# Gated linear attention in a two-layer backbone: running, rescaled q and k instead of operands rebuilt from the gate at each block size

## Chip, cores and metric

The kernel runs on one core of a Trainium2 chip, as one launch in float32 (the large projections split each float32 operand into a high and a low part and multiply three times). The metric is the device time of that launch in microseconds: median 3550.06 us over three runs, 3549.6 to 3558.3 us.

## The reference, cut to what matters

Two layers, each with one combined input projection, four mixers on 256 columns each (mLSTM, Hyena convolution, gated linear attention "GLA", windowed attention) and one output projection, over 256 context and 2048 latent tokens. The change concerns GLA. For each of 4 heads of 64 channels, in both directions in time:

```
b = jnp.cumsum(ab, axis=2)
decay = jnp.exp(jnp.where(tri, b[:, :, :, None, :] - b[:, :, None, :, :], -jnp.inf))
att = jnp.einsum('bhtd,bhsd,bhtsd->bhts', qb, kb, decay)
o = o_inter + jnp.einsum('bhts,bhse->bhte', att, vb)
```

The decay differs per channel, so `att` is not one product of q and k. A kernel can split a chunk into blocks: between two neighbouring blocks of cc tokens the decay factors at their border into one factor for the later tokens and one for the earlier, and a product of q and k, each multiplied by its factor, gives that off-diagonal square. With cc = 64, 32, ... 1 all pairs of a 128-token chunk are covered; the diagonal is q times k itself (counted twice, once per direction).

## The kernel before, in words

Tokens go in 18 tiles of 128. Each layer runs its mixers one after the other; beside the mixing of one, the PE works on the projection of the next. A helper `paced` ties the projection's matmuls to the mixer's: the projection's k-step i waits for a "mark" (a matmul of the mixer) whose number grows in proportion, so the projection is spread over the mixing. A scheduler then writes out one fixed order of instructions per engine, and every engine works its list strictly in order. GLA mixing (`gla_mix`, L934, `gla_chunk`, L954) runs beside the first part of the mLSTM projection (`mlstm_proj`, 27648 of its 46080 cost units; three matmuls of 256 columns, called one group below, are 64 units). The rest of that projection runs beside `mlstm_pre` (gates and states), which follows GLA.

`gla_chunk` handles one 128-token chunk: 18 of them in layer 0, 16 in layer 1. `streams` lets two chunks be written at a time, the second starting when the first has made 8 steps. In a chunk, `bt` holds the cumulative gate for both directions (4 blocks of 128: direction by head pair) and `qk` q and k. For each block size cc = 64 to 2, one level:

- L995 subtracts the gate at the block border from `bt` into `D` (512 elements per partition; DVE for three levels, POOL for three);
- L999 to L1001 exponentiate it into `ex` with the sign that each quarter needs (ACT, 256 + 128 + 128 elements);
- L1002 multiplies `ex` by `qk` (DVE, 512 elements);
- L1008, L1011 or L1015 multiply k by q on the PE. For cc below 32 that is 16 matmuls of 64x32 by 64x32, four column groups by two row groups of the array.

No level reads what another level wrote. Levels cc = 1 and 0 (the diagonal) use L980 to L989. Then the six small results are merged by masks into `D32` (L1022, L1024) and copied into the 128x128 `S` (L1027); L1029 and L1031 make `qi`, q times the decay from the chunk's ends; L1038 to L1042 are the output matmuls; `hh` is copied out of PSUM (L216) and normalised (`head_norm`: POOL square L661, DVE L662, then `rsqrt_mean` L225 to L230 with two ACT steps, L664), multiplied by the SiLU gate and transposed out (L696).

Of the kernel before, what the change touches and what calls it, by code (L numbers as in the profile page):

```python
# [41 lines left out]
def consts():  # L42
# [114 lines left out]
class Net:  # L157
# [796 lines left out]
    def gla_chunk(self, p, c, sb, ngb, sel):  # L954
        nc = self.nc
        qk = p.tile([P, 4, P], F32, tag="qk", name="qk")
        nc.sync.dma_start(out=qk, in_=self.qk_src(self.g_qk, c))
        bt = p.tile([P, 4, P], F32, tag="bt", name="bt")
        nc.sync.dma_start(out=bt, in_=self.g_bt[c])
# [11 lines left out]
        vC = [pS[:, :, x:x + 64].rearrange("p e (m t) -> p e m t", m=2) for x in (256, 320, 384, 448)]  # L971
        vD = [pS[:, 0, x:x + 4].rearrange("p (m e) -> p e m", m=2) for x in (0, 4)]
        for lv, cc in enumerate((64, 32, 16, 8, 4, 2, 1, 0)):
            ex = p.tile([P, 4, P], F32, tag="ex", name="ex", bufs=4)
            if cc < 2:
                if cc:
                    t2 = lambda x, i: x.rearrange("p j (n x) -> p j n x", x=2)[:, :, :, i]
                    D = p.tile([P, 512], F32, tag="D", name="D")
                    Dv = D[:, :256].rearrange("p (j n) -> p j n", j=4)
                    nc.gpsimd.tensor_sub(out=Dv, in0=t2(bt, 1), in1=t2(bt, 0))  # L980
                    for i in range(2):
# [35 lines left out]
            if cc == 32:  # L1017
                nc.scalar.copy(out=S, in_=vS)
# [719 lines left out]
```

## Time and profile before

| | |
|---|---|
| median of 3 runs | 3550.06 us (3549.6 to 3558.3) |
| profiled execution: span, first to last instruction | 3548.5 us |
| what lies around the span | the median run is 1.6 us longer than this span, the fastest 1.1 us |
| busy share PE / DVE / ACT / POOL | 91% / 61% / 40% / 37% |
| mean granted clock of the PE | 0.941 of 2.4 GHz |
| GLA mixing in layer 0 | from 1047 to 1400 us |
| GLA mixing in layer 1 | from 2827 to 3118 us |

The 91% of the PE is an average over stages and counts matmuls whose ends are modelled; a granted clock of 0.5 means that the PE ran at 1.2 GHz. A stage is judged by its own windows: how much of it the PE was busy, at which clock, and which wait ended last there.

### The profile page before, as it was taken

How to read it: one execution, taken by the hardware profiler on the slowest of the kernel's cores; microseconds unless marked ns; L12 is line 12 of the kernel's file. 1: busy time of each engine (PE TensorE's matmuls, PEld its weight loads, DVE VectorE, ACT ScalarE, POOL GpSimd, SP SyncE). 2: the span in 40 equal slices, each digit the busy share in tenths (PEclk: the TensorE clock that was granted, in tenths of full speed). 3: DMA queues.
4: the chain of work that ended last, by engine and by line, in shares of the span. 5: the costliest groups of instructions: out<-in, count | busy, mean ns of one | idle time of the engine just before them, and what ended most of it. 6: DMA issues, size and time to landing. Idle time of an engine off the chain costs nothing. (4 is left out here: it accounts for less than half of the span.)

```text
span 3548.5 us, 68631 instructions
## 1 busy us (share of the span) xinstructions
PE 3243.7 (91%) x24673; PEld 2694.4 (76%) x24673; DVE 2178.6 (61%) x5322; ACT 1424.0 (40%) x4044; POOL 1311.0 (37%) x1561
## 2 busy tenths in 40 slices
PE   6989999899998989988898999998999998887998
PEld 4778878698886778876678677776988876776776
DVE  6733565553458686579888425664533478946887
ACT  5513444332544443233435324443325445522333
POOL 3611111232126565245555421112331266723555
PEclk8999999999998988989899999999999999997999
DMA  6374443684354432475434474435753432237443
GB/s 247 105 209 121 113 116 105 181 248 128 120 174 139 129 116 69 145 221 161 147 124 136 114 209 129 117 98 161 234 153 108 134 89 88 82 100 199 156 146 106
DMA packets 532007, 503.65 MB, mean 142 GB/s; under 512 B 113808, under 2 KB 457677, under 8 KB 531667
## 3 DMA queue, kind: packets, MB, share of 16 engines
q1 hardware_dynamic: 531667, 499.26, 47.2%
q8 instruction: 195, 3.19, 0.4%
q14 instruction: 145, 1.19, 0.1%
HBM read 333.18 MB, written 165.92 MB: 141 GB/s over the span
## 5 line engine op out<-in xcount | busy, mean ns | idle before, releaser
L480 PE MATMUL pp<-w,hi 128*128 128x256 f32 (+2 forms) x1984 | 593.5, 301 | 25.1 <-ACT w L425 11.4
L482 PE MATMUL pp<-w,hi 128*128 128x256 f32 (+2 forms) x1984 | 595.1, 301 | 6.2 <-POOL w L426 6.0
L483 PE MATMUL pp<-w,ho 128*128 128x256 f32 (+2 forms) x1984 | 590.9, 298 | 3.4 <-POOL ho L380 3.2
L463 PE MATMUL pp<-hi,w 128*128 128x512 f32 (+1 forms) x1328 | 526.6, 397 | 5.0 <-ACT w L425 3.2
L466 PE MATMUL pp<-hi,w 128*128 128x512 f32 (+1 forms) x1328 | 515.8, 390 | 1.9 <-POOL w L426 1.7
L465 PE MATMUL pp<-ho,w 128*128 128x512 f32 (+1 forms) x1328 | 515.9, 389 | 0.0
L480 PEld LDWEIGHTS pp<-w,hi 128*128 128x128 f32 x1984 | 388.0, 196 | 45.2 <-ACT w L425 16.9
L482 PEld LDWEIGHTS pp<-w,hi 128*128 128x128 f32 x1984 | 388.8, 196 | 22.3 <-issue 10.3
L483 PEld LDWEIGHTS pp<-w,ho 128*128 128x128 f32 x1984 | 389.4, 196 | 16.7 <-issue 9.0
L426 POOL TENSOR_TENSOR w<-raw,w 128x256 fp32r<-128x256 f32 (+2 forms) x256 | 197.3, 788 | 525.1 <-ACT w L425 487.8
L463 PEld LDWEIGHTS pp<-hi,w 128*128 128x128 f32 x1328 | 257.5, 194 | 62.1 <-issue 9.2
L466 PEld LDWEIGHTS pp<-hi,w 128*128 128x128 f32 x1328 | 253.4, 192 | 53.1 <-POOL w L426 3.3
L465 PEld LDWEIGHTS pp<-ho,w 128*128 128x128 f32 x1328 | 255.5, 192 | 45.3 <-issue 3.2
L1639 PE MATMUL pp<-woh,w 128*128 128x512 f32 x544 | 235.7, 434 | 30.7 <-ACT pp L1643 17.5
L1640 PE MATMUL pp<-wol,w 128*128 128x512 f32 x544 | 224.0, 413 | 0.0
L1641 PE MATMUL pp<-woh,w 128*128 128x512 f32 x544 | 221.2, 416 | 2.1 <-POOL w L1628 2.1
L216 DVE COPY st<-pp 128x256 f32<-128x256 f32 (+2 forms) x152 | 79.5, 523 | 199.2 <-PE pp L483 98.6
L1002 DVE TENSOR_TENSOR ex<-ex,qk 128x512 f32<-128x512 f32 x204 | 180.1, 885 | 30.1 <-ACT ex L1001 27.1
L218 ACT COPY st<-pp 128x256 f32<-128x256 f32 (+2 forms) x152 | 68.6, 451 | 260.8 <-PE pp L483 139.0
L1208 POOL TENSOR_TENSOR sg<-sg,gt 128x256 f32<-128x256 f32 x34 | 25.0, 737 | 396.1 <-ACT sg L654 357.7
L652 ACT ACTIVATE sg<-sg 128x256 f32<-128x256 f32 (+1 forms) x120 | 60.6, 505 | 241.3 <-DVE sg L651 225.5
L425 ACT CAST w<-raw 128x256 fp32r<-128x256 f32 (+2 forms) x256 | 96.3, 407 | 150.4 <-DMA raw<-in_w_in_dram 90.8
(591 smaller groups left out, 7327.0 us busy)
## 6 DMA issues: line engine op xcount, KB each, us to landing
raw<-in_w_in_dram SPq DMA_DIRECT2D x96, 256.0 KB
q<-d_tq SPq DMA_DIRECT2D x68, 256.0 KB
E<-d_mM SPq DMA_DIRECT2D x68, 256.0 KB
d_yraw<-st SPq DMA_DIRECT2D x64, 256.0 KB
raw<-in_w_ada_dram SPq DMA_DIRECT2D x64, 256.0 KB
wsho<-d_aT SPq DMA_DIRECT2D x34, 384.0 KB
kl<-d_tk SPq DMA_DIRECT2D x28, 384.0 KB
d_gbt<-bt SPq DMA_DIRECT2D x36, 256.0 KB
```

The lines of the kernel that those rows point to most:

```text
L425: nc.scalar.copy(out=t[:, 0, :n], in_=raw[:, i, :n])
L426: nc.gpsimd.tensor_sub(out=t[:, 1, :n], in0=raw[:, i, :n], in1=t[:, 0, :n])
L463: mm = nc.tensor.matmul(out=ps[:, :n], lhsT=a, rhs=hi[:, k], start=(k == 0), stop=False)
L465: nc.tensor.matmul(out=ps[:, :n], lhsT=a, rhs=lo[:, k], start=False, stop=False)
L466: nc.tensor.matmul(out=ps[:, :n], lhsT=b, rhs=hi[:, k], start=False, stop=(k == KD - 1))
L480: mm = nc.tensor.matmul(out=ps[:, :n], lhsT=a, rhs=wk[k][:, 0, :n], start=(k == 0), stop=False)
L482: nc.tensor.matmul(out=ps[:, :n], lhsT=a, rhs=wk[k][:, 1, :n], start=False, stop=False)
L483: nc.tensor.matmul(out=ps[:, :n], lhsT=b, rhs=wk[k][:, 0, :n], start=False, stop=(k == KD - 1))
L1002: nc.vector.tensor_mul(out=ex, in0=ex, in1=qk)
L1639: nc.tensor.matmul(out=ps, lhsT=ak[k][:, 0], rhs=hi[:, k], start=(k == order[0]), stop=False)
L1640: nc.tensor.matmul(out=ps, lhsT=ak[k][:, 0], rhs=lo[:, k], start=False, stop=False)
L1641: nc.tensor.matmul(out=ps, lhsT=ak[k][:, 1], rhs=hi[:, k], start=False, stop=(k == order[-1]))
```

## The change

One tile `X` of four quarters (256 elements each: two head pairs by 128 tokens) replaces the levels' separate operands: at first q, k, k, and q times the whole-block factor of the backward direction; quarter 0 is multiplied by the factor of the forward direction. All factors of all levels come from one small tile `A` (1016 elements), filled by seven POOL subtractions of gate values one block apart and two ACT exponentials per chunk. Then the levels run smallest block first: the PE multiplies what `X` holds, and afterwards two DVE multiplications in place scale `X` by the factors of this block size, so that it is ready for the next larger one. For cc = 2 to 32 an ACT copy first gathers the two kinds of k into one tile `KM` (one buffer). After the last level, quarters 0 and 3 of `X` are q times the decay from both chunk ends, so `qi` with its exponential and product goes. The copies of `D32` into `S` move from DVE to ACT. X loads q once and k twice (three DMAs for one), and the gate tile has a gap of one column per block.

```
+        for cc in (1, 2, 4, 8, 16, 32, 64):
+            nc.gpsimd.tensor_sub(out=grid(A, off, (508, 2), (254, 2), (1, n)), in0=grid(T, cc, (257, 2), (129, 2), (cc, n)),
+                                 in1=grid(T, 0, (257, 2), (129, 2), (cc, n)))
+        for d in range(2):
+            nc.scalar.activation(out=A[:, 508 * d:508 * d + 508], in_=A[:, 508 * d:508 * d + 508], func=ACTF.Exp, scale=0.125 * d - 0.0625)
...
+        nc.gpsimd.tensor_mul(out=qk, in0=quad(0), in1=quad(1))
...
+        for d in (1, 0):
+            nc.vector.tensor_mul(out=grid(X, 768 * d, (128, 2), (1, P)), in0=grid(X, 0, (128, 2), (1, P)), in1=grid(A, 508 * d, (254, 2), (1, P)))
-        for lv, cc in enumerate((64, 32, 16, 8, 4, 2, 1, 0)):
+        for cc in (1, 2, 4, 8, 16, 32, 64):
...
-                (nc.vector if lv in (1, 3, 5) else nc.gpsimd).tensor_sub(out=Dv, in0=bv, in1=bv[:, :, cc - 1].unsqueeze(2).to_broadcast([P, 512 // x, x]))
-                nc.scalar.activation(out=self.pair(ev[:, :h, lo], cc), in_=self.pair(Dv[:, :h, lo], 256 + cc), func=ACTF.Exp, scale=0.0625)
-                nc.scalar.activation(out=ev[:, h:, lo], in_=Dv[:, h:, lo], func=ACTF.Exp, scale=-0.0625)
-                nc.scalar.activation(out=ev[:, h:, hi], in_=Dv[:, :h, hi], func=ACTF.Exp, scale=-0.0625)
-                nc.vector.tensor_mul(out=ex, in0=ex, in1=qk)
+            if cc in (1, 64):
+                KM = quad(1)
+            else:
+                KM = p.tile([P, 256], F32, tag="KM", name="KM", bufs=1)
+                nc.scalar.copy(out=grid(KM, 0, (x, 256 // x), (cc, 2), (1, cc)), in_=grid(X, 256, (x, 256 // x), (256 + cc, 2), (1, cc)))
...
+                w = max(32, x)
+                for j in range(0, P, w):
+                    kk = Kr[:, o:o + w]
+                    qq = grid(Xr, o, (x, w // x), (768 + cc, 2), (1, cc))
+                    if cc == 32:
+                        mk = nc.tensor.matmul(out=vS[j:j + 64, e, m, j:j + 64], lhsT=kk, rhs=qq, start=True, stop=True)
+                    else:
+                        mk = nc.tensor.matmul(out=vC[cc][j:j + 32, e, m], lhsT=kk, rhs=qq, start=True, stop=True, tile_position=(64 * e, j))
...
+            if cc < 64:
+                for i, u in ((0, 0), (2, 1)):
+                    t = grid(X, 256 * i + cc * u, (128, 4), (x, b), (1, cc))
+                    nc.vector.tensor_mul(out=t, in0=t, in1=grid(A, f + 1 - u, (254, 4), (2, b), (0, cc)))
+            if cc == 1:
+                nc.vector.tensor_copy(out=D32, in_=vC[1])
+                nc.vector.copy_predicated(out=D32, mask=self.msk[:, 4].unsqueeze(1).unsqueeze(1).to_broadcast([P, 2, 2, 32]),
...
+        nc.scalar.copy(out=S, in_=vS)
...
-            nc.vector.tensor_copy(out=S[x, :, :, x], in_=D32[x])
-        nc.scalar.activation(out=qi, in_=bt, func=ACTF.Exp, scale=0.0625)
-        nc.gpsimd.tensor_mul(out=qv, in0=qv, in1=qk[:, 0:2].unsqueeze(1).to_broadcast([P, 2, 2, P]))
+            nc.scalar.copy(out=S[x, :, :, x], in_=D32[x])
```

The scheduler's lists change with it. On DVE, between the copy of one chunk's `hh` out of PSUM (L216) and the work on the next, layer 0 before:

```order
L995 TENSOR_TENSOR D<-bt 128x512
L216 COPY hh<-pse 128x256
L984 TENSOR_TENSOR ex<-ex 128x256
L1002 TENSOR_TENSOR ex<-ex,qk 128x512 x2
L995 TENSOR_TENSOR D<-bt 128x512
L662 TENSOR_REDUCE ss<-sq 128x4
L1022 COPY D_12752<-psA 128x128
```

The same place in the changed kernel (L998 sets up `X`, L1031 scales it after a level, L1037 and L1038 begin `D32`):

```order
L1044 COPY_PREDICATED D_12597<-msk,psC 128x128 x4
L216 COPY hh<-pse 128x256
L998 TENSOR_TENSOR X<-X,A 128x256
L662 TENSOR_REDUCE ss<-sq 128x4
L998 TENSOR_TENSOR X<-X,A 128x256
L225 TENSOR_SCALAR v<-ss 128x4
L228 SCALAR_TENSOR_TENSOR t<-ss 128x4
L229 TENSOR_TENSOR t<-t,v 128x4
L230 SCALAR_TENSOR_TENSOR ss<-t,ss 128x4
L664 TENSOR_TENSOR hh<-hh,ss 128x256
L1031 TENSOR_TENSOR X<-X,A 128x256 x2
L1037 COPY D_12796<-psA 128x128
```

Before, work of the next chunk's levels stands ahead of the copy of `hh`; now the next chunk's first multiplication stands behind it, and the first scaling of `X` behind the norm of the chunk before.

On PE, the levels of one chunk in layer 0 of the changed kernel (L1024 are the matmuls of a level, L463 to L466 one group of the projection):

```order
L1024 MATMUL psC<-X,KM 32x32 x16
L463 MATMUL pp<-hi_678,w 128x512
L465 MATMUL pp<-ho_679,w 128x512
L466 MATMUL pp<-hi_678,w 128x512
L1024 MATMUL psC<-X,KM 32x32 x16
L463 MATMUL pp<-hi_678,w 128x512
L465 MATMUL pp<-ho_679,w 128x512
L466 MATMUL pp<-hi_678,w 128x512
L1022 MATMUL psC<-X,KM 64x64 x8
```

Before, the matmuls of several levels of a chunk could stand together, as the 48 of three levels here in layer 0, behind the last output matmul of the chunk before:

```order
L1042 MATMUL pse<-sb_10802,qi 128x128
L1015 MATMUL psA<-ex 32x32 x48
L463 MATMUL pp<-hi_678,w 128x512
L465 MATMUL pp<-ho_679,w 128x512
L466 MATMUL pp<-hi_678,w 128x512
L463 MATMUL pp<-hi_678,w 128x512
```

Now two levels are never adjacent: three matmuls of 512 columns, or six of 256, stand between them.

On ACT, the end of one chunk and the start of the next in the changed kernel (L1005 copies into `KM`, L1047 the four copies into `S`, L984 the exponentials of the next chunk, L652 to L654 the sigmoid):

```order
L1005 COPY KM<-X 128x256 x4
L218 COPY st<-pp 128x4x64
L1042 COPY S<-psC 128x512
L1047 COPY S<-D_12995 32x4x32 x4
L984 ACTIVATE A<-A 128x508 x2
L226 ACTIVATE t<-v 128x4
L227 ACTIVATE ss<-t 128x4
L1005 COPY KM<-X 128x256
L652 ACTIVATE sg<-sg 128x256
```

What moved: the four `S` copies now stand on ACT between the last level and the output matmuls.

## Rows read from the trace of the kernel before

**Rows 1.** Busy time by stretch: PE, PEld, DVE, ACT, POOL, granted clock, DMA, GB/s.
```profile
1072.00:1400.00 328.00, 288.96 (x3997) 236.22 (x3988) 251.01 (x501) 148.64 (x511) 211.21 (x243) 0.85 0.39 116
2849.00:3118.00 269.00, 232.11 (x3408) 200.48 (x3382) 224.77 (x425) 130.57 (x445) 187.90 (x217) 0.92 0.29 87
1400.00:1518.00 118.00, 112.70 (x928) 97.91 (x927) 60.01 (x206) 21.21 (x56) 24.49 (x30) 1.00 0.45 133
3118.00:3250.00 132.00, 113.23 (x907) 97.48 (x905) 65.22 (x205) 26.52 (x66) 34.39 (x38) 0.93 0.54 154
```

**Rows 2.** Timeline, DVE: first and last hh copy of each layer (start, duration).
```profile
1071.64 0.43 DVE L216 COPY hh<-pse 128x256 f32<-128x256 f32 x1 [1.71 <-PE pse L1042]
...
1400.34 0.42 DVE L216 COPY hh<-pse 128x256 f32<-128x256 f32 x1 [5.61 <-PE pse L1042]
...
2848.88 0.42 DVE L216 COPY hh<-psm 128x256 f32<-128x256 f32 x1 [1.38 <-PE psm L1042]
...
3118.12 0.42 DVE L216 COPY hh<-psm 128x256 f32<-128x256 f32 x1
```

**Rows 3.** Waits of PE, 1040 to 1400 us, longest first: total, times, longest.
```profile
PE psC L1015 <- DVE ex L1002: 9.2, 5, 3.7
```

**Rows 4.** Timeline, PE, 2.4 GHz: one level; output matmuls; first and last of seven projection matmuls.
```profile
1313.33 0.36 PE L1015 MATMUL psC<-ex 64*32 64x32 f32 x32
...
1310.13 0.56 PE L1041 MATMUL pse<-v,S 128*128 128x64 f32 x4
...
1311.42 0.44 PE L1042 MATMUL pse<-sb,qi 128*128 128x128 f32 x2
...
1317.12 0.28 PE L482 MATMUL pp<-w,hi 128*128 128x256 f32 x1
...
1317.83 0.28 PE L482 MATMUL pp<-w,hi 128*128 128x256 f32 x1
```

**Rows 5.** Line L661 (POOL), line L999 and L1000 (ACT): ns min/median/max.
```profile
L661 POOL TENSOR_TENSOR sq<-hh x68: 606/614/1595, 1073.0 to 3522.9; 128x256 f32<-128x256 f32 x68
L999 ACT ACTIVATE ex<-D x204: 398/417/455, 1044.9 to 3101.4; 128x256 f32<-128x256 f32 x102
L1000 ACT ACTIVATE ex<-D x204: 290/294/325, 1045.2 to 3101.7; 128x128 f32<-128x128 f32 x102
```

**Rows 6.** Timeline, DVE: the norm of one chunk with no other work between.
```profile
1401.49 0.42 DVE L662 TENSOR_REDUCE ss<-sq 128x4 f32<-128x256 f32 x1 [0.40 <-POOL sq L661]
...
1403.21 0.42 DVE L664 TENSOR_TENSOR hh<-hh,ss 128x256 f32<-128x256 f32 x1
```

**Rows 7.** Timeline, DVE: two independent 256-element operations, and five masked copies in a row.
```profile
2984.33 0.41 DVE L664 TENSOR_TENSOR hh<-hh,ss 128x256 f32<-128x256 f32 x1
2984.66 0.41 DVE L216 COPY hh<-psm 128x256 f32<-128x256 f32 x1
...
3107.73 1.65 DVE L1024 COPY_PREDICATED D<-msk,psC 128x128 f32<-128x128 uint8 x5
```

**Rows 8.** Timeline, PE, 1.2 GHz: one level; first and last output matmuls.
```profile
1120.51 0.47 PE L1015 MATMUL psA<-ex 64*32 64x32 f32 x32 [1.72 <-DVE ex L1002]
...
1249.85 0.95 PE L1041 MATMUL pse<-v,S 128*128 128x64 f32 x4
...
1252.30 0.74 PE L1042 MATMUL pse<-sb,qi 128*128 128x128 f32 x2
```

**Rows 9.** Tile ex, whole run: ns min/median/max, first and last start.
```profile
L1002 DVE TENSOR_TENSOR ex<-ex,qk x204: 673/693/1779, 1045.8 to 3103.0; 128x512 f32<-128x512 f32 x102
L1008 PE MATMUL psA<-ex x136: 272/272/579, 1047.1 to 3073.8; 64*128 64x128 f32 x136
```

**Rows 10.** Groups by shape, 2827 to 3118 us, DVE: busy us, mean ns.
```profile
L1002 DVE TENSOR_TENSOR ex<-ex,qk 128x512 f32<-128x512 f32 x95 | 87.5, 924 | 6.7 <-ACT ex L1001 6.2
```

**Rows 11.** Line L984 (DVE, 256 elements, right behind POOL's L983): ns min/median/max.
```profile
L984 DVE TENSOR_TENSOR ex<-ex x34: 410/956/1511, 1056.7 to 3105.0; 128x256 f32<-128x256 f32 x34
```

**Rows 12.** Tile ex, 2815 to 2860 us: first GLA matmul of layer 1.
```profile
L1008 PE MATMUL psA<-ex x16: 272/272/373, 2827.0 to 2858.1; 64*128 64x128 f32 x16
```

More of the change, by code (lines that the diff above doesn't have):

```diff
@@ L952, in pair, with grid, gla_chunk @@
         return bass.AP(ap.tensor, ap.offset, [ap.ap[0], [step, 2], *ap.ap[1:]])
[L954 to L959, printed above, removed]
+    @staticmethod
+    def grid(ap, off, *dims):
+        return bass.AP(ap.tensor, ap.offset + off, [ap.ap[0], *[list(d) for d in dims]])
+    def gla_chunk(self, p, c, sb, T, ngb, sel):
+        nc, grid = self.nc, self.grid
+        X = p.tile([P, 4 * 256], F32, tag="X", name="X")
+        src = self.qk_src(self.g_qk, c)
+        quad = lambda i: X[:, 256 * i:256 * i + 256]
+        nc.sync.dma_start(out=grid(T, 0, (129, 4), (1, P)), in_=self.g_bt[c])
+        for i in range(3):
+            nc.sync.dma_start(out=quad(i).rearrange("p (m t) -> p m t", m=2), in_=src[:, 2:] if i else src[:, :2])
         v = p.tile([P, 256], F32, tag="v", name="v")
@@ new lines, in gla_chunk @@
+        vC = {cc: pS[:, :, x:x + 64].rearrange("p e (m t) -> p e m t", m=2) for cc, x in ((16, 256), (8, 320), (4, 384), (2, 448), (1, 64))}
+        vD = pS[:, 0, 0:4].rearrange("p (m e) -> p e m", m=2)
+        qk = p.tile([P, 256], F32, tag="hh", name="qk")
+        nc.gpsimd.tensor_mul(out=qk, in0=quad(0), in1=quad(1))
+        for m in range(2):
+            mk = nc.tensor.matmul(out=pS[:, 0, 2 * m:2 * m + 2], lhsT=qk[:, P * m:P * m + P], rhs=sel, start=True, stop=True)
+        self.marks.append(mk)
@@ L1020, in gla_chunk @@
             yield
         nc.sync.dma_start(out=gt, in_=self.g_g[c][:, :256])
[L1022 to L1024 removed]
+        nc.scalar.copy(out=S, in_=vS)
+        for i, cc in enumerate((16, 8, 4, 2)):
+            nc.vector.copy_predicated(out=D32, mask=self.msk[:, i].unsqueeze(1).unsqueeze(1).to_broadcast([P, 2, 2, 32]), data=vC[cc])
@@ L1037, in gla_chunk @@
             po = pf.rearrange("p (h d) -> p h d", h=2)
-            nc.tensor.matmul(out=pf, lhsT=qi[:, 2 + m], rhs=sb[:, 0, m].rearrange("p h d -> p (h d)"), start=True, stop=False)
+            nc.tensor.matmul(out=pf, lhsT=X[:, 768 + P * m:768 + P * m + P], rhs=sb[:, 0, m].rearrange("p h d -> p (h d)"), start=True, stop=False)
             for h in range(2):
@@ L1041, in gla_chunk @@
                 nc.tensor.matmul(out=po[:, h], lhsT=S[:, h, m], rhs=v[:, 64 * g:64 * g + 64], start=False, stop=False, skip_group_check=True)
-            nc.tensor.matmul(out=pf, lhsT=qi[:, m], rhs=sb[:, 1, m].rearrange("p h d -> p (h d)"), start=False, stop=True)
+            nc.tensor.matmul(out=pf, lhsT=X[:, P * m:P * m + P], rhs=sb[:, 1, m].rearrange("p h d -> p (h d)"), start=False, stop=True)
         self.copy(hh.rearrange("p h d -> p (h d)"), pq.rearrange("p m n -> p (m n)"))
```

82 lines of the change are left out of this document (31 added, 51 removed).

## Prediction, made before the changed kernel was run

> **What bounds the kernel now.** I read the busy time by stretch first, because the change touches only the two GLA stages. In the one of layer 0 the PE is busy 289 of 328 us at a mean clock of 0.85, in layer 1 232 of 269 us at 0.92; behind each stage it is busy 96% and 86% at 1.00 and 0.93 [rows 1]. So the GLA stages are where PE time is lost, to waits and to the slower clock. DVE and POOL together are busy 462 of 328 us and 413 of 269 us there [rows 1], so they often run at once. Then the copies of `hh` give the pace: 17 chunks in 1400.34 - 1071.64 us, 19.34 us each, in layer 0; 15 in 3118.12 - 2848.88, 17.95 us each, in layer 1 [rows 2]. The PE's waits inside a stage are short, the longest kind 9.2 us in total [rows 3]: no single chain holds the old stage; the levels are independent and fill each other's gaps.
>
> **The change, part by part.** Per chunk it removes, on ACT, three exponentials for each of six levels and `qi`; on DVE, three subtractions of 512 elements, six products of 512 and four copies; on POOL, three subtractions, `qi` and the two levels below 2. It adds twelve DVE products of 256 elements, two of 128 and two of 256 to start, five ACT gathers, two ACT exponentials, four ACT copies, seven POOL subtractions of 1016 elements in all. All engines but the PE have less to do. The PE gets one more level of 16 matmuls and 8 smaller ones for the 4 of cc = 64, and 2 diagonal matmuls in place of 4: about 0 in sum (a level is 0.36 us, [rows 4]). What costs is that the levels are now a chain: PE reads `X`, DVE scales it, ACT gathers `KM`, PE reads again. And by the lists in the section on the change, the next chunk starts on DVE only behind the copy of `hh`. So the pace of a chunk is the length of its chain, P, from one copy of `hh` to the next. The projection cannot fill more than its pace: counted in the list, a steady chunk has 17 to 19 groups, 51 to 57 matmuls of 0.118 us, about 6.5 us, and GLA itself has some 5.5 us on the PE.
>
> P at the fast clock with nothing in the way, handovers between engines 0.05 us each:
> - copy of `hh` 0.42; POOL square 0.61 [rows 5]; the norm from L662 to the end of L664, 1403.21 + 0.42 - 1401.49 = 2.14 [rows 6]; one start product between, 0.3; handovers: 3.6 us.
> - two products of 256 elements: 0.41 each, the second 0.33 later [rows 7], 0.75 us. Level 1 on the PE is hidden beside the norm.
> - levels 2 to 32: gather 0.41, the time of L999 for 256 elements [rows 5]; PE 0.36 [rows 4]; products 0.75; handovers 0.15: 1.67 us, times 5 = 8.35. The sigmoid's three steps on ACT delay the second gather by about 0.35 (an estimate: three of about 0.41 and a copy, less one level). 8.7 us.
> - level 64: PE 0.46 (estimate: two column widths of a level), two products of 128 elements 0.5 (estimate from [rows 7]), four masked copies at 1.65 / 5 = 0.33 each [rows 7], four ACT copies 0.29 with 0.2 between their starts, 0.9 [rows 5], handovers: 3.4 us.
> - output matmuls 1310.13 to 1311.86, 1.73 us [rows 4], and the handover: 1.8 us.
>
> Sum: 18.2 us. The projection's groups between two levels take 6 x 0.118 = 0.7 us and fit beside the 1.3 us in which DVE and ACT work.
>
> Two costs come on top. **The clock:** at P = 18.2 the PE would be busy some 12 of 18 us, less than in the old stage where 88% still meant a mean clock of 0.85 [rows 1]. At 1.2 GHz a level takes 0.47 and the output 1252.30 + 0.74 - 1249.85 = 3.2 us [rows 8], so 7 x 0.11 + 1.46 = 2.2 us more. The ends are 0 and 2.2; I take half, 1.1. **DVE beside POOL:** L1002 takes 673 ns alone and 924 on average in layer 1, where POOL is busy 70% [rows 9, 10, 1], 37% longer. POOL will have about 7 us per chunk (norm and gate as now, seven subtractions, one product), 35%, so half of that on about 6.2 us of products: 1.1 us. The lower end is 0. The upper is six products that each meet a POOL operation at the price of L984, 956 instead of 410 ns [rows 11]: 3.3 us. I take 1.1, as the average holds many meetings. P = 20.4 us.
>
> On these meetings the Trainium skill ("SBUF — State Buffer", "SBUF: two separate sides") says that DVE with two SBUF inputs and GpSimd exclude each other from the port for a whole instruction, which speaks for the upper end: by it the sum would be that of the third rival below. The 956 ns of L984 agree with it [rows 11].
>
> The strided reads of level 1 and 2 are bounded by L999, which reads pairs of pieces, and by twice that; 0.4 us in one level, which I leave at 0 since the level 1 read lies beside the norm. The two extra DMAs of a chunk on SP are issued a chunk ahead (two `X` buffers) and cost nothing while a transfer needs less than 18 us.
>
> **Sum.** Start: between the first GLA matmul and the second chunk the list now holds 75 groups of 272 columns (0.377 us, [rows 4] by the columns) in layer 0, 76 in layer 1, with GLA's own 5.5 us 33.8 and 34.2 us to the first copy of `hh`; it was 1071.64 - 1047.1 = 24.5 and 2848.88 - 2827.0 = 21.9 [rows 2, 9, 12]. GLA begins 8 and 4 groups earlier, 3.0 and 1.5 us. Net 6.3 + 10.8 = 17 us. Pace: 17 (P - 19.34) + 15 (P - 17.95). Given back: at the last level's matmul 488 groups of the projection are done instead of 422, and 490 instead of 448 in layer 1; 108 x 0.355 = 38 us less remain for the stage behind [rows 4, 1]. There DVE has only 60 and 65 us of work in 118 and 132 us, but its gate steps are a chain of their own, so I count three quarters, 28 us (ends 15 and 38). Together 32 P - 609; break-even at P = 19.0. With P = 20.4: +44 us. Against the profiled execution, 3548.5 + 44 = 3592.5 us of span; the median lies 1.6 us above that execution, so **3594 us**.
>
> **Rivals.**
> - *Faster.* The old stage is held by DVE and POOL getting in each other's way; with half the POOL work this ends, the clock stays up, P = 18.2: 582 - 609 = -27, 3523 us. For it: 924 against 673 ns, and all of DVE, ACT and POOL get less. Against: 12 of 18 us of PE work. It decides below P = 18.7. Chance 0.22.
> - *No change.* Only one of the two costs arises: P = 19.3 or less, 617 - 609 = +8, about 3555 us. Chance 0.13.
> - *Much slower.* POOL meets the products at the upper price and the clock is half the time low: P = 18.2 + 3.3 + 1.1 = 22.6, +114, 3664 us. For it: POOL's subtractions for the next chunk stand in the middle of this chunk's levels. Chance 0.12.
>
> **How the numbers follow.** A measurement of this kernel can tell 0.3%, 10.7 us, from no change. The forecast, P from 19.4 to 21.9, has 0.53, and 3562 to 3642 us. Faster by over 0.3% is the first rival, 0.22; within it the second, 0.13; slower 0.53 + 0.12 = 0.65. The range goes to 3524 below, which leaves out half of the first rival, and to 3642 above, which leaves out most of the third: some 2 in 10. The signs hold 0.65 to 0.22, and the forecast's own range is 3562 to 3642.
>
> **What would show it.** Right: copies of `hh` 20 to 21 us apart in both layers; DVE waiting for PE (L1024) and ACT (gathers) before L1031, PE waiting for ACT `KM` at every level; a lower mean clock than 0.85 and 0.92 in the stages; DVE and POOL under half busy; the stage behind GLA shorter by some 28 us in sum. Wrong: a distance under 19 us; products of 256 elements at 0.41 us on average; a PE that waits little. The chain argument falls if PE is still over 85% busy at a clock of 0.9.

## The result, and the profile after

The changed kernel takes 3770.09 us (median of 4 runs, 3758.77 to 3772.17) against 3554.18 us for the kernel before in the same comparison: a ratio of 1.0591, 95% interval 1.0564 to 1.0618. It is slower, as forecast, but by some 216 us instead of 44, and outside the range.

PE is busy 88% of the span (before 91%), DVE 54% (61%), ACT 37% (40%), POOL 30% (37%): every engine but the PE has less to do, and the kernel is longer. Busy time by stretch: the GLA stage of layer 0, that of layer 1, and 118 and 132 us behind each, as in [rows 1]; the columns are those of [rows 1].

```profile
1091.00:1532.00 441.00, 341.23 (x4617) 250.49 (x4615) 184.06 (x536) 134.32 (x353) 124.48 (x232) 0.75 0.30 88
2977.00:3337.00 360.00, 277.44 (x3915) 214.46 (x3914) 158.12 (x461) 114.94 (x300) 104.71 (x199) 0.77 0.23 66
1532.00:1650.00 118.00, 100.28 (x855) 86.96 (x855) 59.43 (x204) 20.28 (x54) 24.14 (x29) 0.93 0.45 127
3337.00:3469.00 132.00, 103.80 (x869) 89.31 (x869) 63.52 (x209) 25.37 (x64) 33.69 (x37) 0.92 0.56 159
```

The stages last 441 and 360 us instead of 328 and 269, at a mean clock of 0.75 and 0.77 instead of 0.85 and 0.92. The stretches behind them, where the PE had been busy 112.70 and 113.23 us, now hold 100 and 104 us of PE work at a lower clock. First and last copy of `hh` in each layer (timeline of DVE; before: [rows 2]):

```profile
1091.44 0.42 DVE L216 COPY hh<-pse 128x256 f32<-128x256 f32 x1 [2.53 <-PE pse L1058]
...
1532.25 0.42 DVE L216 COPY hh<-pse 128x256 f32<-128x256 f32 x1 [3.23 <-PE pse L1058]
...
2977.04 0.42 DVE L216 COPY hh<-psm 128x256 f32<-128x256 f32 x1 [4.63 <-PE psm L1058]
...
3336.85 0.42 DVE L216 COPY hh<-psm 128x256 f32<-128x256 f32 x1 [3.23 <-PE psm L1058]
```

17 chunks in 440.81 us are 25.9 us each (before 19.3), 15 in 359.81 are 24.0 (before 17.9). By these four times the 217.7 us between the two spans (3766.2 and 3548.5) split into: first copy in layer 0 later by 19.8; pace in layer 0, 112.1; last copy of layer 0 to first of layer 1, -3.8; pace in layer 1, 90.6; rest, -1.0. So 203 of 218 us are the pace inside the two stages.

One ordinary chunk of layer 0, DVE (timeline; what is left out is the norm, the masked copies and the sigmoid's first step):

```profile
1407.56 0.42 DVE L216 COPY hh<-pse 128x256 f32<-128x256 f32 x1 [4.75 <-PE pse L1058]
...
1410.11 0.43 DVE L998 TENSOR_TENSOR X<-X,A 128x256 f32<-128x256 f32 x1 [0.87 <-DMA X<-d_gqk]
...
1412.28 1.28 DVE L1031 TENSOR_TENSOR X<-X,A 128x256 f32<-128x256 f32 x2
...
1417.21 0.76 DVE L1031 TENSOR_TENSOR X<-X,A 128x256 f32<-128x256 f32 x2 [1.55 <-PE psC L1024]
1419.21 0.76 DVE L1031 TENSOR_TENSOR X<-X,A 128x256 f32<-128x256 f32 x2 [1.24 <-PE psC L1024]
1421.21 0.76 DVE L1031 TENSOR_TENSOR X<-X,A 128x256 f32<-128x256 f32 x2 [1.24 <-PE psC L1024]
...
1431.18 0.42 DVE L216 COPY hh<-pse 128x256 f32<-128x256 f32 x1 [4.75 <-PE pse L1058]
```

A level comes every 2.00 us, and DVE waits 1.24 us of it for the PE. The PE in the same chunk, two levels with the projection between them and, at the end, the output matmuls:

```profile
1416.54 0.47 PE L1024 MATMUL psC<-X,KM 64*32 64x32 f32 x32
1416.94 0.58 PE L480 MATMUL pp<-w,hi 128*128 128x256 f32 x1
...
1418.17 0.41 PE L483 MATMUL pp<-w,ho 128*128 128x256 f32 x1
1418.54 0.47 PE L1024 MATMUL psC<-X,KM 64*32 64x32 f32 x32
...
1427.79 1.11 PE L1057 MATMUL pse<-v,S 128*128 128x64 f32 x4 [2.24 <-ACT S L1047]
```

These are rows at 1.2 GHz: the level takes 0.47 us [rows 8] and the six projection matmuls fill the 1.6 us to the next one exactly.

Some chunks are much longer: 30 to 40 us for the first three of layer 0, 32.7 and 30.1 for the last of each layer. In these the PE has more of the projection's work between two levels, and DVE waits longer. Rows of DVE in the second chunk of layer 0, where the PE from 1138 to 1152 us is busy 13.12 of 14 us at a clock of 1.00:

```profile
1138.64 0.76 DVE L1031 TENSOR_TENSOR X<-X,A 128x256 f32<-128x256 f32 x2 [4.20 <-PE psA L1024]
1146.42 0.76 DVE L1031 TENSOR_TENSOR X<-X,A 128x256 f32<-128x256 f32 x2 [7.02 <-PE psA L1024]
1151.89 0.76 DVE L1031 TENSOR_TENSOR X<-X,A 128x256 f32<-128x256 f32 x2 [4.71 <-PE psA L1022]
```

Most of the products take as long as alone (tile `X`, ns min/median/max):

```profile
L1031 DVE TENSOR_TENSOR X<-X,A x408: 409/424/1006, 1051.0 to 3328.8; 128x256 f32<-128x256 f32 x136
```

46 of the 408 took over 600 ns, 926 on average, near the 956 that the third rival had priced; each of these began while an instruction of POOL was running.

### The profile page after: what moved, and what is told of

Read it like the earlier page. It is cut to its first block, busy times and chain, and to the rows that moved or that the text cites. A ratio compares the mean times of both kernels' runs of the same rounds, so it can differ in the third digit from the quotient of the medians.

```text
span 3766.2 us, 70875 instructions
## 1 busy us (share of the span) xinstructions
PE 3330.3 (88%) x25897; PEld 2712.9 (72%) x25897; DVE 2023.3 (54%) x5390; ACT 1388.8 (37%) x3704; POOL 1138.6 (30%) x1561
## 3 DMA queue, kind: packets, MB, share of 16 engines
q8 instruction: 205, 3.36, 0.4%
## 5 line engine op out<-in xcount | busy, mean ns | idle before, releaser
L480 PE MATMUL pp<-w,hi 128*128 128x256 f32 (+2 forms) x1984 | 619.7, 314 | 26.3 <-ACT w L425 10.7
L482 PE MATMUL pp<-w,hi 128*128 128x256 f32 (+2 forms) x1984 | 603.2, 304 | 3.3 <-POOL w L426 3.3
L483 PE MATMUL pp<-w,ho 128*128 128x256 f32 (+2 forms) x1984 | 599.6, 303 | 5.1 <-POOL ho L380 5.0
L463 PE MATMUL pp<-hi,w 128*128 128x512 f32 (+1 forms) x1328 | 547.9, 413 | 5.5 <-ACT w L425 4.2
L466 PE MATMUL pp<-hi,w 128*128 128x512 f32 (+1 forms) x1328 | 525.8, 398 | 1.2 <-POOL w L426 0.8
L465 PE MATMUL pp<-ho,w 128*128 128x512 f32 (+1 forms) x1328 | 526.5, 397 | 0.0
L480 PEld LDWEIGHTS pp<-w,hi 128*128 128x128 f32 x1984 | 398.5, 201 | 50.6 <-issue 13.5
L483 PEld LDWEIGHTS pp<-w,ho 128*128 128x128 f32 x1984 | 401.4, 202 | 17.1 <-issue 8.8
L482 PEld LDWEIGHTS pp<-w,hi 128*128 128x128 f32 x1984 | 401.5, 202 | 14.4 <-issue 7.0
L463 PEld LDWEIGHTS pp<-hi,w 128*128 128x128 f32 x1328 | 261.7, 197 | 61.5 <-issue 6.5
L1031 DVE TENSOR_TENSOR X<-X,A 128x256 f32<-128x256 f32 x408 | 178.8, 480 | 235.6 <-PE psC L1024 89.6
L466 PEld LDWEIGHTS pp<-hi,w 128*128 128x128 f32 x1328 | 259.6, 196 | 56.1 <-POOL w L426 3.6
L216 DVE COPY st<-pp 128x256 f32<-128x256 f32 (+2 forms) x152 | 79.6, 524 | 197.1 <-PE pp L483 97.9
L980 POOL TENSOR_TENSOR A<-bt 128x512 f32<-128x512 f32 (+6 forms) x238 | 94.8, 435 | 276.2 <-DVE X L1035 271.8
L1005 ACT COPY KM<-X 128x256 f32<-128x256 f32 x170 | 70.0, 412 | 252.2 <-DVE X L1031 248.8
```

The lines of the kernel that those rows point to most:

```text
L463: mm = nc.tensor.matmul(out=ps[:, :n], lhsT=a, rhs=hi[:, k], start=(k == 0), stop=False)
L465: nc.tensor.matmul(out=ps[:, :n], lhsT=a, rhs=lo[:, k], start=False, stop=False)
L466: nc.tensor.matmul(out=ps[:, :n], lhsT=b, rhs=hi[:, k], start=False, stop=(k == KD - 1))
L480: mm = nc.tensor.matmul(out=ps[:, :n], lhsT=a, rhs=wk[k][:, 0, :n], start=(k == 0), stop=False)
L482: nc.tensor.matmul(out=ps[:, :n], lhsT=a, rhs=wk[k][:, 1, :n], start=False, stop=False)
L483: nc.tensor.matmul(out=ps[:, :n], lhsT=b, rhs=wk[k][:, 0, :n], start=False, stop=(k == KD - 1))
```

## The experiments

The theory: the pace is the serial chain of one chunk, which is longer than I had summed ("chain theory"). The rivals: the PE's own load at a low clock sets the pace ("slow-PE theory"); DVE and POOL get in each other's way ("port theory"). All times below are medians; the changed kernel is 3770.09. Pace means the mean distance of the copies of `hh` in layer 0 and layer 1, 25.9 and 24.0 us in the changed kernel. Ratios are to the kernel before in the same comparison; its median lay between 3554 and 3561 us from one comparison to the next, so a difference of a few us between two experiments says nothing.

### The bare chain

```
-            self.paced(ml, [m for m in gs[LG[6]:] for _ in range(LG[7])] + gx, 27648, LG[8])
+            self.paced(ml, gx[-1:], 27648)
```

> The part of the projection that ran beside GLA mixing is held back until the last GLA level, so that the chain of levels runs by itself. The time of the whole kernel must grow, since about 2 x 150 us of projection now stand behind the stages (3850 to 4000 us); what counts is the distance of the copies of hh. Chain theory: still 19 to 23 us, though the PE has under 10 us of work per chunk. Slow-PE theory: 14 us or less, as the PE's queue is then free.

Measured: 4003.16 us (one run). In layer 1 all distances are 22.4 to 22.8 us, in layer 0 22.5 to 23.3 behind a first one of 32.1. The PE in the two stages (windows):

```profile
1080.00:1475.00 395.00, 169.35 (x3717) 132.50 (x3710) 176.43 (x516) 114.22 (x305) 103.68 (x190) 0.50 0.19 55
3091.00:3430.00 339.00, 141.64 (x3239) 115.06 (x3238) 154.13 (x450) 99.43 (x266) 90.13 (x165) 0.50 0.17 48
```

It is busy 43% and 42% of the time, at 1.2 GHz throughout, and the pace is still 22.6 us. That rules out the PE's load as what sets the least distance: the bare chain is 22.6 us long. One chunk of it, on DVE, then on POOL and on the PE (timelines):

```profile
3182.22 0.42 DVE L216 COPY hh<-psm 128x256 f32<-128x256 f32 x1 [4.75 <-PE psm L1058]
...
3184.68 0.43 DVE L998 TENSOR_TENSOR X<-X,A 128x256 f32<-128x256 f32 x1 [0.78 <-DMA X<-d_gqk]
...
3185.09 0.76 DVE L1031 TENSOR_TENSOR X<-X,A 128x256 f32<-128x256 f32 x2
...
3187.18 1.86 DVE L1031 TENSOR_TENSOR X<-X,A 128x256 f32<-128x256 f32 x2
...
3190.28 0.76 DVE L1031 TENSOR_TENSOR X<-X,A 128x256 f32<-128x256 f32 x2 [1.03 <-PE psC L1024]
3192.25 0.76 DVE L1031 TENSOR_TENSOR X<-X,A 128x256 f32<-128x256 f32 x2 [1.21 <-PE psC L1024]
...
3198.00 0.49 DVE L1035 TENSOR_TENSOR X<-X,A 128x128 f32<-128x128 f32 x2 [0.81 <-PE psC L1013]
...
3204.71 0.43 DVE L216 COPY hh<-psm 128x256 f32<-128x256 f32 x1 [4.75 <-PE psm L1058]
```

```profile
3187.18 0.72 POOL L665 TENSOR_TENSOR hh<-hh,ngb 128x256 f32<-128x256 f32 x1 [3.73 <-DVE hh L664]
3187.98 0.79 POOL L1065 TENSOR_TENSOR hh<-hh,sg 128x256 f32<-128x256 f32 x1
```

The two products of the pair at 3187.18 each (line L1031 in that window, ns min/median/max):

```profile
L1031 DVE TENSOR_TENSOR X<-X,A x2: 943/970/996, 3187.2 to 3188.1; 128x256 f32<-128x256 f32 x2
```

The PE:

```profile
3183.03 0.47 PE L1024 MATMUL psC<-X 64*32 64x32 f32 x32 [0.20 <-DVE X L998]
...
3191.59 0.47 PE L1024 MATMUL psC<-X,KM 64*32 64x32 f32 x32 [1.50 <-ACT KM L1005]
...
3201.32 1.11 PE L1057 MATMUL psm<-v,S 128*128 128x64 f32 x4 [1.97 <-ACT S L1047]
```

Against the terms of the prediction, at the fast clock with nothing in the way; the last column is the mean of the 13 distances between the fourth and the seventeenth copy of `hh` in layer 0 of the changed kernel, called its middle chunks below:

| from, to | forecast us | bare chain us | changed kernel us |
|---|---|---|---|
| copy of `hh`, first product behind level 1 | 3.6 | 2.87 (0.78 a wait for a load) | 4.74 |
| to the products of level 64 | 0.75 + 8.7 + 0.46 = 9.9 | 12.91 | 13.14 |
| to the first output matmul that needs `S` | 2.9 | 3.32 | 3.36 |
| to the next copy of `hh` | 1.8 | 3.39 | 2.40 |
| sum | 18.2 | 22.49 | 23.64 |

In the bare chain the products of level 1 stand ahead of the end of the norm (L664), in the changed kernel behind it, so the first line is shorter there. In the second line of the bare chain one pair of products takes 1.86 us instead of 0.76. Its two products take 1.00 and 0.94 us instead of 0.42, and each began while a product of POOL was running, the first beside L665, the second beside L1065; the other products of this chunk do not meet POOL. On these two meetings the trace agrees with the Trainium skill ("SBUF — State Buffer", "SBUF: two separate sides"), by which DVE with two SBUF inputs and GpSimd exclude each other for a whole instruction: 1.10 us more. Most of the rest of that line is the level, which comes five times: 1.97 us instead of 1.67 (3192.25 - 3190.28).

### The wait for a load

On DVE the first product L998 of a chunk's `X` stands between two steps of the norm, and it is not the next chunk's but that of the chunk after next. The instruction list of the changed kernel, with the buffer numbers of `X` (12566 is the chunk that has just ended):

```
L1035 TENSOR_TENSOR X_12566<-X_12566,A_12576 128x2x64 x2
L1044 COPY_PREDICATED D32_12597<-msk_337,psC_12599 128x128 x4
L216 COPY hh_12785<-pse_12786 128x256
L998 TENSOR_TENSOR X_12765<-X_12765,A_12775 128x256
L662 TENSOR_REDUCE ss_12832<-sq_12831 128x4
L998 TENSOR_TENSOR X_12964<-X_12964,A_12974 128x256
L225 TENSOR_SCALAR v_12835<-ss_12832 128x4
```

`X_12964` reuses the buffer that the output matmuls have just freed, so its load starts only then, and the norm and the next chunk's levels wait behind it: in layer 0 for 16.5 us in 15 waits, in layer 1 for 14.8. The trace shows the same: the matmuls of the next chunk's level 1 start at 3183.03 above, behind the first L998 and 1.65 us ahead of the second. So what stands behind the copy of `hh` is the second start product of the next chunk, whose first one came a chunk earlier, and not, as I had written ahead of the prediction, its first.

```
-        X = p.tile([P, 4 * 256], F32, tag="X", name="X")
+        X = p.tile([P, 4 * 256], F32, tag="X", name="X", bufs=3)
```

(and `bufs=1` for `v`, `D32` and `S`)

> X gets a third buffer (S, v and D32 go down to one each to make room, which a serial chain should not feel). In the changed kernel the first product of the chunk after next stands in the DVE list between two steps of the norm, and waits there for a load that can only start when the last output matmul has freed its X buffer. Chain theory: this wait of 0.8 to 1.7 us per chunk goes, 31 chunks, 30 to 50 us less: 3720 to 3745 us. Slow-PE theory: no change, 3760 to 3780 us.

Measured: 3734.38 us, 36 us less; ratio 1.0503 (1.0476 to 1.0529); pace 25.0 and 22.4. The wait for the load is gone, since that product now stands ahead of the copy of `hh`, where DVE waits for the output matmuls anyway (timeline of DVE; the L998 shown is that of the next chunk):

```profile
3097.22 0.41 DVE L216 COPY hh<-psm 128x256 f32<-128x256 f32 x1
3097.55 0.41 DVE L998 TENSOR_TENSOR X<-X,A 128x256 f32<-128x256 f32 x1
3098.46 0.42 DVE L662 TENSOR_REDUCE ss<-sq 128x4 f32<-128x256 f32 x1 [0.51 <-POOL sq L661]
3098.92 0.17 DVE L225 TENSOR_SCALAR v<-ss 128x4 f32<-128x4 f32 x1
3099.00 1.29 DVE L1031 TENSOR_TENSOR X<-X,A 128x256 f32<-128x256 f32 x2
```

### The end of the chain

```
+            if cc in (2, 4, 8, 16):
+                i = (16, 8, 4, 2).index(cc)
+                nc.vector.copy_predicated(out=D32, mask=self.msk[:, i].unsqueeze(1).unsqueeze(1).to_broadcast([P, 2, 2, 32]), data=vC[cc])
...
-        for i, cc in enumerate((16, 8, 4, 2)):
-            nc.vector.copy_predicated(out=D32, mask=self.msk[:, i].unsqueeze(1).unsqueeze(1).to_broadcast([P, 2, 2, 32]), data=vC[cc])
```

> Each masked copy into D32 stands directly behind its own level's scaling instead of all four behind level 64. The work is the same; four copies of 0.33 us leave the end of the chain. Chain theory: 1.3 us less per chunk, 34 chunks, 44 us less: about 3726 us, with copies of hh 1.3 us closer. Slow-PE theory: no change, 3760 to 3780 us.

Measured: 3692.03 us, 78 us less; ratio 1.0382 (1.0358 to 1.0406); pace 24.0 and 22.2. On ACT the copies into `S` now follow one another; in the changed kernel there were 1.42 us of waiting for `D32` between them (timelines of ACT, first the changed kernel, then this one):

```profile
1424.51 0.59 ACT L1042 COPY S<-psC 128x512 f32<-128x512 f32 x1 [2.02 <-PE psC L1013]
1426.52 1.22 ACT L1047 COPY S<-D 32x128 f32<-32x128 f32 x4 [1.42 <-DVE D L1044]
```

```profile
3106.55 0.59 ACT L1045 COPY S<-psA 128x512 f32<-128x512 f32 x1 [2.80 <-PE psA L1013]
3107.18 1.22 ACT L1048 COPY S<-D 32x128 f32<-32x128 f32 x4
```

The block from the first to the end of the last copy is 1.85 instead of 3.23 us; the gain per chunk was 1.8 to 1.9, more than these 1.4. The other half microsecond is in the output: from its first matmul that needs `S` to the copy of `hh` the middle chunks take 1.87 us instead of 2.40, as long as at a granted clock of 1.00 (1.86 in the experiment on the clock below). Next, the output matmuls in another order, the four that need `S` last for both head pairs:

```
+            nc.tensor.matmul(out=pf, lhsT=X[:, P * m:P * m + P], rhs=sb[:, 1, m].rearrange("p h d -> p (h d)"), start=False, stop=False, skip_group_check=True)
+        for m in range(2):
...
-                nc.tensor.matmul(out=po[:, h], lhsT=S[:, h, m], rhs=v[:, 64 * g:64 * g + 64], start=False, stop=False, skip_group_check=True)
-            nc.tensor.matmul(out=pf, lhsT=X[:, P * m:P * m + P], rhs=sb[:, 1, m].rearrange("p h d -> p (h d)"), start=False, stop=True)
+                nc.tensor.matmul(out=po[:, h], lhsT=S[:, h, m], rhs=v[:, 64 * g:64 * g + 64], start=False, stop=True, skip_group_check=True)
```

> The two output matmuls of each head pair that need only X and the states go first, the four that need S last, so that three of them leave the path from the last copy into S to the copy of hh. Those three take 0.96 + 0.53 = 1.5 us there at 1.2 GHz. Chain theory: 1.5 us less per chunk, 34 chunks, 50 us less, about 3720 us. If the PE's own load set the pace: no change, 3760 to 3780 us.

Measured: 3713.94 us, 56 us less; ratio 1.0452 (1.0417 to 1.0488); pace 23.5 and 21.2. Both gains are about what the chain theory asked for or more; work off the chain's end is time off the kernel. Then three of these edits in one kernel (the wait is taken away here by an order constraint on L998 instead of a third buffer):

> Serial as in the changed kernel, with three parts of the chain's end and start taken off it at once: early masked copies, the output matmuls that need S last, and the first product of the chunk after next kept behind the next chunk's last level, so that it does not wait in the norm for its load. Chain theory: the gains add, 2.2 + 1.5 + 1.0 = 4.7 us a chunk, 33 chunks, 155 us less: 3600 to 3630 us. If something else takes over as the chain gets shorter (projection groups in front of a level): about half of it, 3690 us.

Measured: 3660.98 us, 109 us less; ratio 1.0300 (1.0269 to 1.0331); pace 22.8 and 20.6. That lies between the two expectations; the three single gains add up to 170. Two reasons for the difference can be read from the traces. Two of the edits take away the same wait: with the matmuls that need `S` last, `X` is free earlier, and the order of the output alone had lowered the waits for the load from 31 to 16 us. And the long first and last chunks stay long (30, 35, 29 and at the end 33 us in layer 0, 30 at the end of layer 1), as there the PE is busy with the projection. In the middle chunks the projection hardly takes over: the distance falls by 3.6 us to 20.0, and the stretch of the levels takes 13.5 us instead of 13.1.

### The clock

```
+            pf = self.psp.tile([P, 512], F32, tag="pp", name="pp")
+            for i in range({1: 12, 64: 8}.get(cc, 6)):
+                self.after(nc.tensor.matmul(out=pf[:, :P], lhsT=self.ident, rhs=self.ident, start=True, stop=True), mk, "fill")
```

(on top of the bare chain)

> no_projection with matmuls of the identity (128x128, result never read) behind every level: 12 behind level 1, 6 behind levels 2 to 32, 8 behind level 64. They add no wait to the chain as long as they take less than the gap (1.2 us of the 1.5 us gap between levels at the full clock, by 0.2 us each), and keep the PE busy. It splits the 22.6 us of the bare chain into a part that is the PE at 1.2 GHz and a part that is not. Chain theory with the clock as a part: the granted clock goes up from 0.50, and the distance of the copies of hh falls by up to 2.2 us (output 1.87 instead of 3.39 us, levels 64 and 32 0.25 and 0.12 us less, five levels 0.07 us each), to 20.4 to 21.2 us. If the PE's order matters instead (whatever stands between two levels delays them): 23 to 26 us, although the clock is up.

Measured: 3968.98 us (one run). The PE is now busy 86% and 87% of the stages, and the clock is up (windows):

```profile
1080.00:1458.00 378.00, 324.95 (x5371) 288.78 (x5370) 162.72 (x509) 114.99 (x303) 103.64 (x189) 0.96 0.21 59
3070.00:3400.00 330.00, 286.47 (x4742) 259.52 (x4742) 143.27 (x450) 100.40 (x266) 90.85 (x165) 0.95 0.18 51
```

The distances are 20.7 to 24 us behind a first one of 26.2, and 22.0 on average in layer 1, only 0.6 less than in the bare chain: neither expectation is met cleanly. One chunk shows both sides: the output takes 1.86 us (3203.41 to the copy at 3205.27) instead of 3.39, but the load's wait is longer, and the level is still 1.93 us.

```profile
3208.82 0.42 DVE L998 TENSOR_TENSOR X<-X,A 128x256 f32<-128x256 f32 x1 [1.87 <-DMA X<-d_gqk]
...
3216.07 0.76 DVE L1034 TENSOR_TENSOR X<-X,A 128x256 f32<-128x256 f32 x2 [1.15 <-PE psC L1024]
3218.00 0.76 DVE L1034 TENSOR_TENSOR X<-X,A 128x256 f32<-128x256 f32 x2 [1.17 <-PE psC L1024]
```

The 0.6 us is not the worth of the clock, since the added matmuls cost time of their own. Those behind level 1 (L1028) last 4.5 us, and in the next chunk level 2 waits for their end, though its `KM` has been ready for 1.0 us (ACT, then PE):

```profile
3231.10 0.43 ACT L1005 COPY KM<-X 128x256 f32<-128x256 f32 x1 [0.22 <-DVE X L1034]
```

```profile
3228.10 4.52 PE L1028 MATMUL pp<-ident 128*128 128x128 f32 x24
3232.55 0.36 PE L1024 MATMUL psA<-X,KM 64*32 64x32 f32 x32
```

From the products of level 1 to those of level 2 it takes 2.3 to 4.5 us in 20 of the 32 distances. In the other 12 it takes 2.03 us (2.09 in the bare chain), and these distances are 20.7 to 21.7 us, 21.2 on average, the upper end of the first expectation. So the clock is worth some 1.4 us of the 22.6. The slow clock is a consequence of the chain more than its cause: with the clock back, over nine tenths of the length stays.

### Two chains in flight

If one chain sets the pace, a second one beside it must help.

```
-X_D = (2, 8)
+X_D = (2, 4)
```

(the number of chunks in flight, and the steps of one before the next starts; and two `KM`, one `S`, here and in the kernels below)

> The second of two chunks starts after 4 steps of the first instead of 8, with two KM buffers (and one S buffer, to make room). Chain theory (the pace is the serial chain of one chunk, about 24.9 us on average): by the instruction lists two chunks now share one norm and one start, and the second one's levels run beside the first one's masked copies and output; a pair should take 33 to 38 us, 17 to 19 us a chunk, so 33 x 6 to 8 us less, 3510 to 3580 us. Slow-PE theory (the PE, at about three quarters of its clock and 79% busy in the two stages, sets the pace): the PE's own 18.8 us per chunk stay, so not under 19 to 20 us a chunk and 3590 to 3620 us. Port theory (DVE and POOL in each other's way): more meetings, no gain, 3740 us or more.

Measured: 3679.29 us; ratio 1.0342 (1.0319 to 1.0366). A gain of 91 us, a third to a half of what was expected. The distances alternate, about 15 and 27 us: with two streams the next chunk may start when one has ended, so the stagger is 4 and 8 steps in turn, and each pair still runs mostly in series. With `X_D = (2, 6)` the stagger is even:

> As overlap, but the second chunk starts after 6 steps of 12, so that the stagger is the same for every chunk instead of 4 and 8 in turn. Chain theory: two chains of some 23 us run half a length apart, at least 12 us a chunk; with the PE's own work (13 us at the full clock, 18.8 as measured in the changed kernel) the pace should be 15 to 19 us, 3490 to 3610 us. Slow-PE theory: no better than overlap (21.6 us on average, 3679 us). Port theory: products that meet POOL get longer, 3680 us or more.

Measured: 3610.61 us; ratio 1.0152 (1.0112 to 1.0192); pace 20.4 and 18.9. 160 us of the 216 are back, by the start of the second stream and the second `KM` that it needs. The second `KM` was not run alone; in the bare chain each gather starts 0.1 us behind the DVE products, when the PE has been done with the `KM` before for about 1 us, so a single chain should gain nothing by it. The time is at the upper edge of what the chain theory gave. The port theory is right that products meet POOL more often here, 120 of the 408 take over 600 ns instead of 46, but the kernel is 160 us faster all the same. With the edits of tail_short on top:

> overlap_even and tail_short together. Chain theory: 14 to 17 us a chunk, now near the PE's own load, and 3440 to 3540 us, under the kernel before. If the engines in order (DVE behind POOL, the PE behind its projection groups) hold it: 3550 to 3650 us.

Measured: 3623.14 us; ratio 1.0191 (1.0157 to 1.0226): no gain. With the output order alone:

> overlap_even and out_last together. Chain theory: with two chains in flight a chain that is 1.5 us shorter gives half of it, 0.75 us a chunk, 25 us less than overlap_even: about 3585 us. If the PE's own load and clock hold it: like overlap_even, 3600 to 3620 us.

Measured: 3574.01 us; ratio 1.0063 (1.0038 to 1.0088); pace 19.2 and 17.8, that of the kernel before [rows 2]. And with the order constraint on L998 again:

> overlap_out, with the first product of X kept behind the last level matmul written before it, so that no wait for a load stands in the DVE list. Chain theory: another 0.5 us a chunk, 3570 us. If that product was useful early in the overlap (it fills gaps there): 3590 to 3620 us.

Measured: 3601.26 us; ratio 1.0115 (1.0076 to 1.0153). Holding that product back costs some 27 us in the overlapped kernel (the two intervals just touch), which fits the second expectation: early, it fills gaps there. overlap_tail is this kernel with the early masked copies, and it is 22 us slower still (1.0191 against 1.0115). So two of the three edits that help a single chain do not help beside a second one.

### Projection in the first and last chunks

```
-                self.paced(ml, gx[-LG[9]:] + mp, 18432, LG[10])
+                self.paced(ml, gx[-1:] + mp, 18432, LG[10])
```

> In the changed kernel the second part of the projection (18432 units) was paced by the last 9 marks of GLA and those of the stage behind; here by the last one of GLA, so that none of it stands between the last chunk's levels (56 groups there now). If the last chunk's 30 to 33 us are projection in front of the levels, it falls to 22 to 24 us in both layers, some 8 to 10 us each. If the stage behind takes that work without getting longer (it gave nothing back either when it had less): 14 to 20 us less, 3750 to 3756 us. If the work only moves: the last chunk gets shorter and the time stays, 3765 to 3772 us.

Measured: 3772.23 us; ratio 1.0586 (1.0560 to 1.0613). The last chunk falls from 32.7 and 30.1 to 23.8 and 25.1 us, and the time stays. Projection between the last levels moves work and costs nothing; I had taken those long chunks for a loss. The same edit on overlap_out:

> overlap_out with the edit of held_end; the last chunk there takes 27 to 29 us. If it costs time: 3574 - 15 to 20 = 3554 to 3560 us, level with the kernel before. If the work only moves: 3570 to 3578 us.

Measured: 3570.82 us; ratio 1.0034 (1.0018 to 1.0050): within 4 us of overlap_out, again only moved. On top of it, the marks of the GLA states counted 3 times instead of 6 (`range(LG[7])` becomes `range(3)`):

> overlap_out_end with the marks of the GLA states counted 3 times instead of 6, so that fewer units of the projection are due before GLA mixing and more are spread over its chunks (by the list 48 instead of 71 groups in the first two chunks of layer 0, 40 instead of 91 in layer 1). If the late start is that backlog: the first copy of hh comes 5 to 15 us earlier, and 3540 to 3550 us, under the kernel before. If the later chunks pay for it (20 to 22 groups each instead of 17): 3555 to 3575 us.

Measured: 3558.95 us; ratio 0.9989 (0.9974 to 1.0004). The first copy of `hh` comes at 1083.74 instead of 1091.36 us, and the pace grows to 19.0 and 18.3. The stages (windows):

```profile
1084.00:1407.00 323.00, 278.81 (x4512) 215.71 (x4504) 184.35 (x534) 130.39 (x351) 126.84 (x232) 0.86 0.42 121
2850.00:3124.00 274.00, 237.27 (x3866) 196.14 (x3866) 168.19 (x455) 114.68 (x309) 115.29 (x207) 0.86 0.32 91
```

These read like [rows 1]: nearly the same lengths (323 and 274 us) and PE shares, with the clock 0.06 lower in layer 1, and far less DVE and POOL work. The change, overlapped, is as fast as the kernel before and not faster; what holds it at this pace was not tested.

### The kernel before, with one edit

> The kernel before, with its output matmuls in the order of out_last: the same 1.5 us leave the end of a chunk. If the old stage is not held by one chain (its levels are independent and fill each other's gaps): no change within 0.5%, 3540 to 3570 us. If it is held by a chain too: 34 x 1.5 = 50 us less, about 3505 us.

Measured: 3547.85 us; ratio 0.9969 (0.9953 to 0.9985). The same kernel once more, in one comparison with the last two overlapped kernels:

> Control: before_out_last a second time, in the same call as the two overlapped kernels, to compare with them on one chip: 3540 to 3555 us, 0.3% under the kernel before.

Measured: 3541.24 us; ratio 0.9952 (0.9937 to 0.9966). This is the fastest of all kernels here, 11 and 20 us under the kernel before in the two comparisons. It is no chain effect of 50 us: the pace is 19.5 and 17.8 against 19.3 and 17.9 before. In the first of the two profiles the stage of layer 1 ends 9.7 us earlier (last copy of `hh` at 3108.39), most of which it is ahead when the stage begins (first copy 2841.89, 7.0 earlier). Why that is I did not find out.

## Why the prediction was right in its sign and wrong in its size

**Right.** The levels are a chain, and the chain sets the pace: the bare chain of 22.6 us at a PE that is idle more than half the time, the gains from every edit at its end, and the 160 us that a second chain gives back show it. DVE waits for the PE before most L1031, the clock falls, and most products take 0.42 us. The third rival's price came about (926 against 956 ns), but for 46 products instead of the 204 that six per chunk make. One sign failed: the PE waits for `KM` at every level only in the bare chain; in the changed kernel the projection fills that time. The first rival (port contention relieved) found its premise, DVE and POOL both less busy, and not its result.

**Wrong, the pace: P = 20.4 us.** This is the step that failed: the chain was summed too short. P measured 25.0 on average, 32 x 4.6 = 148 of the 174 us by which the forecast missed (217.7 against 44). The middle chunks take 23.6, so 3.2 of the 4.6 us are the chain itself: 2.1 in the stretch of the levels (13.1 us against 9.9 and the 1.1 for POOL) and 1.1 at the start (4.7 against 3.6). The other 1.4, 45 us in sum, are the five long first and last chunks. Its terms:

- *Handovers of 0.05 us.* No row of the kernel before stands behind this figure. A level was summed to 1.67 us; it is 1.97 in the bare chain and 1.93 with the clock up. By the rows of a level, DVE starts 0.67 us behind the start of the PE's level at 1.2 GHz (3191.59 to 3192.25) and 0.60 with the clock up, where I had 0.36 and a handover, 0.41: the clock apart, some 0.2 us more, five times. The gather starts 0.1 us behind the products instead of 0.05.
- *"The ends are 0 and 2.2; I take half, 1.1."* In the bare chain the PE is at 1.2 GHz all the time, and the clock is worth 1.4 us there, most of it in the output. In the middle chunks of the changed kernel the output takes 2.4 us, between 1.86 with the clock up and 3.39 at 1.2 GHz; it depends on the chunk, and the ordinary one above has its output at 1.2 GHz. There half was not far off.
- *"The two extra DMAs of a chunk ... cost nothing."* The transfers are short enough, but I looked at the transfer and not at where the waiting instruction stands. The list quoted ahead of the prediction shows L998 twice behind the copy of `hh`; I read both as the next chunk's. It cost 31 us of waits, and 36 us came back with a third buffer.
- *"DVE beside POOL", 1.1 us* was near in size, by luck: I had taken half a price on all products. What came was nearly the full price on a few, 0.7 us per chunk in the changed kernel and 1.0 in the bare chain.
- *"The projection's groups ... fit beside the 1.3 us."* At 1.2 GHz they take 1.6 us and fill the gap to the last tenth, and a level comes every 2.00 us with them and 1.97 without; but the groups are not spread evenly, and this makes the long chunks. For the last chunks held_end shows that this only moves work; for the first ones it was tried only in the overlapped kernel, where less backlog brought 12 us (3570.82 to 3558.95). How much of the 45 us is loss in the changed kernel stays open.

**Wrong, the start: 17 us.** The first copy of `hh` is 19.8 us later in layer 0. In layer 1, from the first GLA matmul (L995, at 2936.91) it takes 40.1 us against 21.8, with the start itself 22 us nearer to the last copy of layer 0. That is some 37 us instead of 17. In layer 0 the PE is busy 42.5 of the 46.2 us from the first GLA matmul to the copy, where I had summed 33.8 in all: the projection takes 31 us instead of 28, and 9 us are matmuls of another step (L266) that I had left out. In layer 1 it is busy 36.7 of 40.1 us, 31 of them with the projection. **Given back: 28 us** was near: those 22 us less the 1.5 of the earlier start, and 1.0 behind layer 1, 21.5 in sum.

## What to carry to other kernels

Before a set of independent steps is replaced by a chain with less work in it, write out the chain from one fixed instruction to the same one of the next tile, with every handover between engines taken from rows of the trace (start to start), and at the slow clock if the PE is left waiting. If it is longer than the present pace, the change needs a second chain in flight from the beginning; here the start of the second stream, with a second `KM`, was worth 160 us, and three edits inside the chain together 109. And in an instruction list, look up which buffer an instruction works on: two equal rows may belong to different tiles, and the later one's wait is paid by the earlier.

## What the runs showed of the hardware that I had not expected

- A PE that is busy 42 to 43% of a stage in short pieces stayed at a granted clock of 0.50 for 395 and 339 us on end. With useless matmuls between the levels the mean rose to 0.96 and 0.95, and the chunks that these did not delay got only 6% shorter (22.6 to 21.2 us).
- Start to start, a level of 0.36 us on the PE (0.47 at 1.2 GHz) and the product behind it are 0.60 and 0.67 us apart; a copy on ACT behind a pair of DVE products starts 0.1 us after its end, and the PE 0.05 us after that copy.
- Two DVE products in a row that each began while a POOL product was running took 1.00 and 0.94 us instead of 0.42, together 1.86 us instead of 0.76. All 64 of the 408 products of the bare chain that took over 600 ns began beside a running POOL instruction; a POOL busy 26 to 27% of the two stages cost 1.0 us per chunk by them.
